# Fox scores and all value products on full rows and columns, masks in fp32r, banks cleared by VectorE, all operands at one residue modulo 256 bytes

## The chip, the cores and the metric

The kernel runs on one core of a Trainium2 chip. The metric is the device time in microseconds (us) of one execution. TensorE (PE) multiplies matrices, VectorE (DVE), ScalarE (ACT) and GpSimd (POOL) work element by element, SyncE (SP) issues loads. PEld is PE's loading of weights, the stationary operand of a product; the other operand streams through the array, column by column.

## The reference

A trunk of two layers on 512 frames of 1,024 numbers, in fp32. Layer 0 has two groups of heads side by side: 8 heads of latent attention (MLA) and 8 heads of stick-breaking attention. Layer 1 has 16 heads of forgetting attention, called Fox here. After each mixer come a layer norm, a gated feed-forward (SwiGLU, 2,816 wide), another norm, and a gated embedding.

```python
# stick-breaking, one query block
past = s[None, :] < t[:, None]
z = einsum('bhqd,bhkd->bhqk', q_blk, k) * SB_DIM ** -0.5
log_rem = where(past, log_sigmoid(-z), 0.0)
between = cumsum(log_rem, axis=3, reverse=True) - log_rem
att = where(past, exp(log_sigmoid(z) + between), 0.0)
o = einsum('bhqk,bhkd->bhqd', att, v)
# forgetting attention (Fox), one query block
causal = s[None, :] <= t[:, None]
logits = einsum('bhqd,bhkd->bhqk', q_blk, k) * FOX_DIM ** -0.5 + d_t[..., :, None] - dcum[..., None, :]
w = softmax(where(causal, logits, -inf))
o = einsum('bhqk,bhkd->bhqd', w, v)
# each mixer: x = LN(alpha x + mixer(x)); x = LN(alpha x + SwiGLU(x)); x = x + sigmoid(gate(x)) * embedding
```

## The kernel before

PE works in a rounded fp32 type, fp32r. To keep the accuracy of fp32 each operand is split in a high and a low part (whi and wlo for weights, xTh and xTl for the transposed x, pth and ptl for the transposed weights of an attention), and each product is the sum of three: high by low, high by high, low by high (mm3). In a name such as ps_h<-xTl,whi the tile before the arrow is the bank of PSUM that is written, and the others are what is read.

The attentions put the two parts of 64-wide heads side by side. The queries of a head are a tile of 128 rows: the high part in the head's own 64 rows and the low part in the other 64. The keys of the head have the high part in both halves. So one pass of 128 rows (the second pass) gives two of the three products. The third, high query by low key, is the low pass: it takes the low keys kl, which lie in the head's own 64 rows only, and so contracts 64 rows. Both passes are qk_products. One kl tile of [128, 512] holds the low keys of both heads of a pair, 64 rows each.

A causal mask is added on PE as one more product: the identity times a tile with large negative numbers where the mask forbids. Identity (identb) and masks are bf16. For values (add_values) one product has 128 weight columns, the high and the low part of a head's values, and streams pth; the next has 64 columns, the high part alone, and streams ptl into rows 0 to 63 of the same bank. finish_head adds the two halves of the bank.

A stick-breaking head adds into a part of its bank with each key block, so the bank is cleared first: by a product of 512 columns with a tile of zeros.

One Fox unit is a head and a query block of 128 (16 heads x 4 = 64 units): scores, one step later its softmax (DVE, ACT), later the transposes (PE) and the products with the values. An MLA unit is the same without the bias. Fox handles two heads as a pair, whose queries and keys are projected by project_qk one pair ahead. In the gaps between the steps, fill generators hand PE dense products: projections (ps_qkT, ps_v) and outputs (ps_y). The order on each engine is made when the program is built. Tiles come from pools: kl, pth and ptl take turns in the seven buffers of "pT"; a tile has to wait for the last read of the one before it in its buffer.

Constants and long-lived tiles (identity, masks, neg_tri, neg_ones, x, xTh, xTl) are laid one after another in SBUF, and the pools (pieces of weights, qkT, kl, gT, oT, pth, ptl) behind them. Among them are two tiles of one fp32 column, minus_half and bf, that take 32 bytes each. In the built program xTh and xTl begin at 160 modulo 256 bytes, identity, masks and neg tiles at 128, and every tile of the pools at 192.

Of the kernel before, what the change touches and what calls it, by code (L numbers as in the profile page):

```python
# [10 lines left out]
BF16 = mybir.dt.bfloat16  # L11
# [4 lines left out]
P = 128  # L16
S = 512
NT = S // P
# [14 lines left out]
HD = 64  # L33
# [3 lines left out]
# From here on softplus(z) is z in float32, and exp(z) is still finite.  # L37
SOFT_CAP = 60.0

# Column offsets of the blocks of a causal [rows, keys] map that is stored without its empty part.  # L40
# [6 lines left out]
def trunk(ctx: ExitStack, tc: tile.TileContext, a, out):  # L47
# [13 lines left out]
    # ---------------------------------------------------------------- buffers  # L61
# [23 lines left out]
    # ---------------------------------------------------------------- constants  # L85
    ident = const.tile([P, P], F32, name="ident")
    make_identity(nc, ident)
    identb = const.tile([P, P], BF16, name="identb")
    nc.gpsimd.tensor_copy(identb, ident)

    def mask_tile(name):
        t = const.tile([P, P], BF16, name=name)
        nc.gpsimd.memset(t, 0.0)
        return t

    # [query, key]: keys after the query
    mask_fox = mask_tile("mask_fox")
    nc.gpsimd.affine_select(mask_fox, mask_fox, [[-1, P]], ALU.is_ge, NEG, 0, 1)
    # [key, query]: keys at or after the query
    mask_sb = mask_tile("mask_sb")  # L100
    nc.gpsimd.affine_select(mask_sb, mask_sb, [[1, P]], ALU.is_gt, NEG, 0, -1)
    zeros = mask_tile("zeros")
# [5 lines left out]
    # [key', key]: -1 where key' >= key  # L108
# [3 lines left out]
    minus_half = const.tile([P, 1], F32, name="minus_half")  # L112
# [6 lines left out]
    # ---------------------------------------------------------------- helpers  # L119
    def split(hi, lo, src, scale=1.0, eng=None):  # L120
        """hi + lo == scale * src, each with 12 significant bits."""
        if isinstance(scale, float) and scale == 1.0:
            nc.scalar.copy(hi, src)
            (eng or nc.vector).tensor_tensor(lo, src, hi.bitcast(F32), ALU.subtract)
        else:
            nc.scalar.mul(hi, src, scale)
            nc.vector.scalar_tensor_tensor(lo, src, scale, hi.bitcast(F32), ALU.mult, ALU.subtract)

    # engines that take the high and the low part of weights in turn
# [6 lines left out]
    def wload(src, n, m):  # L136
        """A weight piece [128, n x m] as its two parts, each [128, n, m]."""
# [49 lines left out]
    def layer_norm(t, sums, g, b):  # L187
        """x[t] normalised in place; sums are those of its halves."""
# [22 lines left out]
    def row_weights(w, rows):  # L211
        """Whole rows of weights, as addressed by project_block."""
        pieces = [row_piece(w, r) for r in rows]
        return lambda i, half: both(pieces[i], lambda v: v[:, 0, half * S:(half + 1) * S])

    def project_block(t, lhs, w, first, ps_of, sums=(None, None), halves=(0, 1)):
        """x[t] (+)= [lhs tiles]^T @ w; w(i, half) are the two parts of the weights. A generator, one step per half."""
# [8 lines left out]
    def store_values(ps):  # L226
        """8 heads of values of one token block, per head the two parts side by side: [128, 8 x (64 | 64)]."""
# [5 lines left out]
    def store_part(vals, t, part, ps):  # L233
        """Keeps 4 heads of values of a token block: vals[t, part // 2] holds 8 heads."""
# [5 lines left out]
    def x_values(vals, part, src, ps_of, more=None):  # L240
        """4 heads of values, all frames: vals[frame block, part // 2] holds 8 heads. A generator.
        more, of columns [frame, block, n], takes the products with the further columns of src."""
# [13 lines left out]
    # ---------------------------------------------------------------- work for the gaps of the attention  # L256
    class Fill:
        """Generators of matrix products, emitted a little at a time between the steps of an attention."""
# [48 lines left out]
    def project_qk(dst, hp, i, src, kind, twice):  # L307
        """Transposed, split queries (i = 0, scaled) or keys (i = 1) of two heads, from rows 0:64 and 64:128.

        dst[hp][:, j] has both parts of the queries of head j, the high one in its own rows; dst[hp][:, 2 + j]  # L310
        twice the high part of its keys (the copy by twice[j]); low_keys has the low part in its own rows."""
# [4 lines left out]
        else:  # L316
            low_keys[kind, hp] = act.tile([P, S], F32R, tag="pT", bufs=7, name="kl")
# [6 lines left out]
        for j in range(2):  # L324
# [5 lines left out]
            else:  # L330
# [5 lines left out]
                dve.tensor_tensor(low_keys[kind, hp][own], ps[own], hi.bitcast(F32), ALU.subtract)  # L336

    def qk_products(o, kind, hp, q, k, j, keys_first):
        """The three products of the parts of q and k, each (tile, column, slice), of head j of two, in two passes."""
        own = slice(j * HD, (j + 1) * HD)  # L340
        (qt, qc, qs), (kt, kc, ks) = q, k
        passes = [(qt[own, qc, qs], low_keys[kind, hp][own, ks]), (qt[:, qc, qs], kt[:, kc, ks])]
# [4 lines left out]
    def project_out(w_out, fours, outs, first):  # L347
        """Adds the heads of outs to x: w_out[half, c] are the weights of four heads, outs[2 c] and outs[2 c + 1]."""
# [14 lines left out]
    def finish_rows(lhs, w, first, norm, between=lambda t: None, after=lambda t: None):  # L363
        """The last addend of x, its norm, and the transposes; between(t) emits work for the waits."""
# [17 lines left out]
    def split_pair(both_heads, room=None):  # L382
        """The two parts; in room[0] and room[1] where x^T isn't needed any more."""
# [12 lines left out]
    def add_values(o_ps, kb, pt, val, h, first, last):  # L396
        """Adds a key block: rows 0:64 take both parts of pt with the high part of val, 64:128 its low part."""
        th, tl = pt
        c = h * 2 * HD
        nc.tensor.matmul(o_ps[:, kb * P:], lhsT=val[:, c:c + 2 * HD], rhs=th, start=first, stop=False,  # L400
                         skip_group_check=True)
        nc.tensor.matmul(o_ps[0:HD, kb * P:], lhsT=val[:, c:c + HD], rhs=tl, start=False, stop=last,
                         skip_group_check=True)

    # ---------------------------------------------------------------- softmax attention
# [3 lines left out]
    def softmax_attention(n_pairs, head, mask, outs, fill, ns, kind, norm_engines, room):  # L409
        """head(hp, j) gives scores(qb, ps), bias(qb) or None, values by key block, and the head among them.  # L410

        Step by step: scores of one query block; its weights one step later; their transposes five, and the
        products with the values six steps later. norm_engines by query block; room gives places of outs."""
# [22 lines left out]
        def scores(u):  # L436
# [10 lines left out]
            if mask is not None:  # L447
                nc.tensor.matmul(u.s[:, u.n - P:u.n], lhsT=identb, rhs=mask, start=False, stop=True)

        def weights(u):  # L450
# [6 lines left out]
            else:  # L457
# [3 lines left out]
                # the row's own term, in the maximum as in the logits  # L461
# [44 lines left out]
    # ---------------------------------------------------------------- stick-breaking attention  # L506
    def stick_attention(n_pairs, pair, vals, outs, fill, ns, kind, room):
        """pair(hp) gives the projected queries and keys of two heads; vals are the value blocks.

        Scores are kept [key, query]; key blocks run from the last to the first. Step by step: softplus of  # L510
        one block, one step later its weights, and three steps later their products with the values."""
# [11 lines left out]
        def scores(u):  # L523
# [5 lines left out]
            nc.tensor.matmul(u.z[:, 0:P], lhsT=identb, rhs=mask_sb, start=False, stop=True)  # L529
# [575 lines left out]
```

## Time and profile before

| | |
|---|---|
| time, median of 3 runs | 1426.98 us (1425.24 to 1427.11) |
| span of the profiled execution | 1425.5 us |
| PE busy | 1396.9 us, 98% of the span |
| DVE, ACT, POOL busy | 56%, 43%, 28% |

The profile gives the span of one execution; the runs give a time each. The first attention (MLA and stick-breaking) ends around 282 us, the feed-forward and gate of layer 0 run to about 736, the Fox attention to about 960, and the feed-forward of layer 1 to the end.

### The profile page before, as it was taken

The numbers are of one execution on the slowest core, as the hardware profiler recorded it, in microseconds if no ns is written. First come the engines' busy times: TensorE is split into PE (matmuls) and PEld (weight loads), VectorE is DVE, ScalarE is ACT, GpSimd is POOL, SyncE is SP. The second block draws the span as 40 slices with busy tenths as digits, with TensorE's granted clock in tenths as the row PEclk, the third lists the DMA queues.
The fourth block names the chain that finished last, engine by engine and source line by source line (L and its number), as shares of the span: only waits on it lengthen the run. The fifth ranks groups of instructions, "written<-read, shape, count | busy, mean of one in ns | idle before, by whom it ended". The sixth has DMA issues, their size and how long they took to land.

```text
span 1425.5 us, 18859 instructions
## 1 busy us (share of the span) xinstructions
PE 1396.9 (98%) x6784; PEld 1129.2 (79%) x6784; DVE 793.8 (56%) x1481; ACT 607.3 (43%) x1261; POOL 401.9 (28%) x400
## 2 busy tenths in 40 slices
PE   8999999799999999999989999999999999999998
PEld 7888777588888888887877788778888888888877
DVE  4655789833444444448636665698434444444485
ACT  4666776542322232324446564665422223232242
POOL 5654732221111111112144443442211111111130
PEclk9999999999999999999999999999999999999999
DMA  6211412142232333331233222122423232322212
GB/s 229 91 41 40 129 53 89 60 133 74 89 102 93 104 101 97 96 103 60 83 116 111 79 81 68 45 82 92 138 74 103 92 105 92 106 94 95 98 60 96
DMA packets 69166, 131.75 MB, mean 92 GB/s; under 512 B 8128, under 2 KB 8896, under 8 KB 69056
## 3 DMA queue, kind: packets, MB, share of 16 engines
q1 hardware_dynamic: 66304, 120.75, 26.3%
q0 software_dynamic: 2768, 9.80, 2.0%
q8 instruction: 53, 0.87, 0.3%
q14 instruction: 41, 0.34, 0.1%
HBM read 127.80 MB, written 2.72 MB: 92 GB/s over the span
## 4 chain that ended last, share of the span: by engine, by line
PE 91%; DVE 4%; DMA 2%; ACT 2%; issue 1%; SPq 0%; POOL 0%; DVEq 0%; POOLq 0%; ACTq 0%
PE ps_h L151 12%; PE ps_h L153 12%; PE ps_h L152 12%; PE ps_y L151 7%; PE ps_y L152 7%; PE ps_y L153 7%; PE ps_s L345 3%; PE ps_qkT L151 3%; PE ps_qkT L152 3%; PE ps_qkT L153 3%; PE ps_g L153 2%; PE ps_g L151 2%; PE ps_g L152 2%; PE ps_t L434 2%; PE ps_z L539 1%; PE ps_v L151 1%
## 5 line engine op out<-in xcount | busy, mean ns | idle before, releaser
L147 POOL TENSOR_TENSOR wlo<-wraw,whi 128x512 fp32r<-128x512 f32 (+2 forms) x212 | 276.6, 1312 | 777.4 <-ACT whi L146 648.4
L146 ACT CAST whi<-wraw 128x512 fp32r<-128x512 f32 (+1 forms) x402 | 237.7, 616 | 577.4 <-PE ps_h L152 263.6
L152 PE MATMUL ps_h<-xTh,whi 128*128 128x512 f32 (+1 forms) x736 | 283.9, 386 | 0.0
L151 PE MATMUL ps_h<-xTl,whi 128*128 128x512 f32 (+1 forms) x736 | 283.9, 386 | 0.0
L153 PE MATMUL ps_h<-xTh,wlo 128*128 128x512 f32 (+1 forms) x736 | 283.8, 386 | 0.0
L147 DVE TENSOR_TENSOR wlo<-wraw,whi 128x512 fp32r<-128x512 f32 (+1 forms) x215 | 172.1, 816 | 134.9 <-ACT whi L146 133.3
L209 DVE TENSOR_TENSOR x<-x,ps_y 128x512 f32<-128x512 f32 x176 | 119.8, 683 | 151.8 <-PE ps_y L153 151.7
L153 PEld LDWEIGHTS ps_h<-xTh,wlo 128*128 128x128 f32 x736 | 138.3, 188 | 30.4
L152 PEld LDWEIGHTS ps_h<-xTh,whi 128*128 128x128 f32 x736 | 138.3, 188 | 30.2
L151 PEld LDWEIGHTS ps_h<-xTl,whi 128*128 128x128 f32 x736 | 138.2, 188 | 30.3
L152 PE MATMUL ps_y<-whi,gT 128*128 128x512 f32 x352 | 137.1, 390 | 0.0
L151 PE MATMUL ps_y<-wlo,gT 128*128 128x512 f32 x352 | 137.1, 391 | 0.0
L153 PE MATMUL ps_y<-whi,gT 128*128 128x512 f32 x352 | 136.2, 389 | 0.0
L666 DVE TENSOR_TENSOR silu<-silu,ps_h 128x512 f32<-128x512 f32 x44 | 30.3, 688 | 121.8 <-PE ps_h L153 119.4
L151 PE MATMUL ps_qkT<-xTl,whi 128*128 128x512 f32 x192 | 79.1, 412 | 2.1 <-DVE fu L916 0.9
L152 PE MATMUL ps_qkT<-xTh,whi 128*128 128x512 f32 x192 | 77.6, 404 | 0.0
L151 PEld LDWEIGHTS ps_y<-wlo,gT 128*128 128x128 f32 x352 | 66.1, 188 | 14.4
L153 PE MATMUL ps_qkT<-xTh,wlo 128*128 128x512 f32 x192 | 77.4, 403 | 0.0
L153 PEld LDWEIGHTS ps_y<-whi,gT 128*128 128x128 f32 x352 | 66.1, 188 | 14.2
L152 PEld LDWEIGHTS ps_y<-whi,gT 128*128 128x128 f32 x352 | 66.1, 188 | 14.2
L151 PE MATMUL ps_v<-wlo,xTh 128*128 128x256 f32 (+1 forms) x192 | 56.4, 295 | 3.3 <-DVE wlo L147 3.2
L152 PE MATMUL ps_v<-whi,xTh 128*128 128x256 f32 (+1 forms) x192 | 55.2, 289 | 0.0
(234 smaller groups left out, 2513.0 us busy)
## 6 DMA issues: line engine op xcount, KB each, us to landing
wraw<-in_ffn_w_dram SPq DMA_DIRECT2D x264, 256.0 KB, 2.8
wraw<-in_w_gate_dram SPq DMA_DIRECT2D x32, 256.0 KB, 2.9
wraw<-in_w_qkf_dram SPq DMA_DIRECT2D x32, 256.0 KB, 2.9
wraw<-in_w_qkb_dram SPq DMA_DIRECT2D x16, 256.0 KB, 3.0
wraw<-in_a_w_out_dram SPq DMA_DIRECT2D x16, 256.0 KB, 2.7
kbias<-nd_dram POOLq DMA_DIRECT2D x8, 512.0 KB, 5.0
wraw<-in_c_w_out_dram SPq DMA_DIRECT2D x16, 256.0 KB, 2.9
wraw<-in_w_vf_dram SPq DMA_DIRECT2D x15, 256.0 KB, 3.1
```

What stands on the lines that cost most here:

```text
L146: (eng_hi.copy if eng_hi is acts else eng_hi.tensor_copy)(hi[:, c:end], raw)
L147: eng_lo.tensor_tensor(lo[:, c:end], raw, hi[:, c:end].bitcast(F32), ALU.subtract)
L151: nc.tensor.matmul(o, lhsT=lhs[0], rhs=rhs[1], start=first, stop=False)
L152: nc.tensor.matmul(o, lhsT=lhs[0], rhs=rhs[0], start=False, stop=False)
L153: nc.tensor.matmul(o, lhsT=lhs[1], rhs=rhs[0], start=False, stop=last)
L209: nc.vector.tensor_tensor(xs, xs, ps, ALU.add)
L345: nc.tensor.matmul(o, lhsT=lhsT, rhs=rhs, start=n == 0, stop=False)
L434: nc.tensor.transpose(u.ps[:, blk(qb - u.i)], u.h.pr[:, QOFF[qb] + u.i * P:QOFF[qb] + (u.i + 1) * P], ident)
L539: nc.tensor.matmul(u.z[:, c:u.n], lhsT=w, rhs=rhs, start=False, stop=i == len(mms) - 1, skip_group_check=True)
L666: nc.vector.tensor_tensor(s, s, hps[1], ALU.mult)
```

## The change

It has five parts. No computation of the reference is left out; where 128 rows or columns take the place of 64, a product of two low parts is added to the sum.

1. The identity and the masks are fp32r (identr, mask_fox, mask_sb); each is built in a scratch tile and copied. The transposes read identr as fp32.
2. The stick-breaking bank is cleared by a memset of VectorE.
3. For Fox (both_halves), each head of a pair has its own kl tile. Its own 64 rows are written as before and then copied to the other 64, by ACT for the first head and by GpSimd for the second. The low pass contracts 128 rows. The stick-breaking heads keep one kl tile for each pair and 64 rows.
4. Both value products have 128 weight columns.
5. minus_half and bf become columns of a tile of 32 fp32 (128 bytes). In the built program xTh, xTl, x and every tile of the pools then begin at 0 modulo 256 bytes; identr, masks, neg tiles and the columns tile begin at 128.

```diff
+LINE = 32
-    ident = const.tile([P, P], F32, name="ident")
-    make_identity(nc, ident)
-    identb = const.tile([P, P], BF16, name="identb")
-    nc.gpsimd.tensor_copy(identb, ident)
+    identr = const.tile([P, P], F32R, name="identr")
+    raw_ident = temp("scratch")[:, 0:P]
+    make_identity(nc, raw_ident)
+    nc.vector.tensor_copy(identr, raw_ident)
+    ident = identr.bitcast(F32)
-    def mask_tile(name):
-        t = const.tile([P, P], BF16, name=name)
-        nc.gpsimd.memset(t, 0.0)
+    def mask_tile(name, *select):
+        raw = temp("scratch")[:, 0:P]
+        nc.gpsimd.memset(raw, 0.0)
+        nc.gpsimd.affine_select(raw, raw, *select)
+        t = const.tile([P, P], F32R, name=name)
+        nc.vector.tensor_copy(t, raw)
-    zeros = mask_tile("zeros")
-    minus_half = const.tile([P, 1], F32, name="minus_half")
+    columns = const.tile([P, LINE], F32, name="columns")
+    minus_half = columns[:, 0:1]
...
-            low_keys[kind, hp] = act.tile([P, S], F32R, tag="pT", bufs=7, name="kl")
+            low_keys[kind, hp] = [act.tile([P, S], F32R, tag="pT", bufs=7, name="kl") for _ in range(1 + both_halves)]
...
-                dve.tensor_tensor(low_keys[kind, hp][own], ps[own], hi.bitcast(F32), ALU.subtract)
+                low = low_keys[kind, hp][j if both_halves else 0]
+                dve.tensor_tensor(low[own], ps[own], hi.bitcast(F32), ALU.subtract)
+                if both_halves:
+                    (acts.copy if j == 0 else gps.tensor_copy)(low[other], low[own].bitcast(F32))
...
-        passes = [(qt[own, qc, qs], low_keys[kind, hp][own, ks]), (qt[:, qc, qs], kt[:, kc, ks])]
+        low = low_keys[kind, hp]
+        rows, low = (slice(0, P), low[j]) if len(low) == 2 else (slice(j * HD, (j + 1) * HD), low[0])
+        passes = [(qt[rows, qc, qs], low[rows, ks]), (qt[:, qc, qs], kt[:, kc, ks])]
...
-        nc.tensor.matmul(o_ps[:, kb * P:], lhsT=val[:, c:c + 2 * HD], rhs=th, start=first, stop=False,
-                         skip_group_check=True)
-        nc.tensor.matmul(o_ps[0:HD, kb * P:], lhsT=val[:, c:c + HD], rhs=tl, start=False, stop=last,
-                         skip_group_check=True)
+        for n, t in enumerate(pt):
+            nc.tensor.matmul(o_ps[:, kb * P:], lhsT=val[:, c:c + 2 * HD], rhs=t, start=first and n == 0,
+                             stop=last and n == 1, skip_group_check=True)
...
-                nc.tensor.matmul(u.s[:, u.n - P:u.n], lhsT=identb, rhs=mask, start=False, stop=True)
+                nc.tensor.matmul(u.s[:, u.n - P:u.n], lhsT=identr, rhs=mask, start=False, stop=True)
...
-            nc.tensor.matmul(u.z[:, 0:P], lhsT=identb, rhs=mask_sb, start=False, stop=True)
+            nc.tensor.matmul(u.z[:, 0:P], lhsT=identr, rhs=mask_sb, start=False, stop=True)
...
-                nc.tensor.matmul(h.o_ps, lhsT=zeros,
-                                 rhs=zeros.rearrange("p (o m) -> p o m", o=1).broadcast_to([P, NT, P]),
-                                 start=True, stop=False, skip_group_check=True)
+                nc.vector.memset(h.o_ps, 0.0)
...
-        bf = const.tile([FOX_H, 1], F32, name="bf")
+        bf = columns[0:FOX_H, 1:2]
```

What the change moves in the order: the first piece is PE in the Fox attention, one unit's scores with a value projection around it, before:

```order
L345 MATMUL ps_s<-kl,qkT 128x512
L345 MATMUL ps_s<-qkT 128x512
L448 LDWEIGHTS identb
L448 MATMUL ps_s<-mask_fox,identb 128x128
L151 MATMUL ps_v<-wlo,xTh 128x256
L152 MATMUL ps_v<-whi,xTh 128x256
L153 MATMUL ps_v<-whi,xTl 128x256
L402 MATMUL ps_o<-ptl,val 64x512
L400 MATMUL ps_o<-pth,val 128x384
```

and the same unit in the changed kernel, where the line numbers are those of its own code:

```order
L353 MATMUL ps_s<-kl,qkT 128x512
L408 MATMUL ps_o<-pth,val 128x512
L353 MATMUL ps_s<-qkT 128x512
L454 MATMUL ps_s<-mask_fox,identr 128x128
L155 MATMUL ps_v<-whi,xTh 128x256
L156 MATMUL ps_v<-whi,xTl 128x256
L408 MATMUL ps_o<-ptl,val 128x512
L440 MATMUL ps_t<-identr,prob 128x128
L408 MATMUL ps_o<-pth,val 128x384
```

The mask has no weight load of its own row any more, ptl's product writes 128 rows of the bank where it wrote 64, and a product of pth has moved in between the two passes.

The second piece is ACT in the Fox attention of the changed kernel, around the keys of a pair (L335 and L339 write the high keys, L343 the copy of the low keys of the first head):

```order
L470 ACTIVATE prob,sm<-prob,nb 128x512
L335 CAST qkT<-ps_qkT 64x512
L339 CAST qkT<-ps_qkT 64x512
L343 CAST kl<-kl 64x512
L335 CAST qkT<-ps_qkT 64x512
L126 CAST val<-ps_v 128x4x64
L126 CAST pth<-ps_t 128x128
```

L343 is new; what stood behind it stands behind it still.

The third piece is DVE in the stick-breaking attention of the changed kernel, where a head's bank is cleared (sp is the softplus of the scores ps_z, val the low part of values):

```order
L388 TENSOR_TENSOR o<-ps_o,o_low 64x512
L577 TENSOR_SCALAR sp<-ps_z 128x512
L127 TENSOR_TENSOR val<-ps_v,val 128x4x64
L552 MEMSET ps_o 128x512
L577 TENSOR_SCALAR sp<-ps_z 128x128
L587 TENSOR_TENSOR sp<-ps_z,sp 128x512
```

The memset is new on DVE, between the end of one head (L388) and the softplus of a later block; the other rows stand as before.

## Rows read from the trace of the kernel before

**Rows 1.** The page: the chain that ended last, by engine.
```profile
PE 91%; DVE 4%; DMA 2%; ACT 2%; issue 1%; SPq 0%; POOL 0%; DVEq 0%; POOLq 0%; ACTq 0%
```

**Rows 2.** Windows: start:end, length, busy us (count) by engine, PE's granted clock, DMA share, GB/s.
```profile
12.00:228.00 216.00, 214.09 (x1203) 174.40 (x1202) 142.63 (x289) 137.05 (x336) 115.05 (x113) 1.00 0.28 87
228.00:282.00 54.00, 45.45 (x210) 33.55 (x208) 44.85 (x100) 31.31 (x75) 10.67 (x14) 0.94 0.23 73
282.00:700.00 418.00, 417.47 (x1879) 341.06 (x1878) 197.02 (x281) 133.15 (x232) 74.45 (x67) 1.00 0.30 95
746.00:960.00 214.00, 213.64 (x1157) 165.12 (x1156) 142.93 (x413) 123.29 (x299) 91.21 (x91) 1.00 0.24 80
```

**Rows 3.** Timeline of PE, three streams' ends: start us, us, engine, line, out<-in, shapes.
```profile
330.02 0.40 PE L151 MATMUL ps_h<-xTl,whi 128*128 128x512 f32 x1
...
336.79 0.40 PE L153 MATMUL ps_h<-xTh,wlo 128*128 128x512 f32 x1
...
337.25 0.39 PE L152 MATMUL ps_y<-whi,gT 128*128 128x512 f32 x1
...
339.52 0.39 PE L153 MATMUL ps_y<-whi,gT 128*128 128x512 f32 x1
...
680.18 0.39 PE L152 MATMUL ps_g<-whi,xTh 128*128 128x512 f32 x1
...
682.51 0.39 PE L153 MATMUL ps_g<-whi,xTl 128*128 128x512 f32 x1
```

**Rows 4.** Timeline of PE, a Fox unit behind an output product.
```profile
900.84 0.39 PE L153 MATMUL ps_y<-whi,oT 128*128 128x512 f32 x1
901.16 0.49 PE L345 MATMUL ps_s<-kl,qkT 64*128 64x512 f32 x1
901.58 0.50 PE L345 MATMUL ps_s<-qkT 128*128 128x512 f32 x1
901.92 0.23 PE L448 MATMUL ps_s<-mask_fox,identb 128*128 128x128 bf16 x1
901.96 0.48 PE L400 MATMUL ps_o<-pth,val 128*128 128x512 f32 x1
902.28 0.40 PE L402 MATMUL ps_o<-ptl,val 128*64 128x512 f32 x1
902.51 0.34 PE L400 MATMUL ps_o<-pth,val 128*128 128x384 f32 x1
```

**Rows 5.** Lines by shape, PE: count | busy us, mean ns | idle before.
```profile
L152 PE MATMUL ps_h<-xTh,whi 128*128 128x512 f32 x672 | 265.8, 396 | 0.0
L152 PE MATMUL ps_qkT<-xTh,whi 128*128 128x512 f32 x192 | 77.6, 404 | 0.0
L152 PE MATMUL ps_g<-whi,xTh 128*128 128x512 f32 x120 | 47.5, 396 | 0.0
```

**Rows 6.** Lines by shape, DVE and POOL, in the projection of keys.
```profile
L336 DVE TENSOR_TENSOR kl<-ps_qkT,qkT 64x512 fp32r<-64x512 f32 x24 | 16.4, 685 | 9.5 <-ACT qkT L335 6.8 <-ACT qkT L331 2.5
L333 POOL CAST qkT<-qkT 64x512 fp32r<-64x512 f32 x8 | 4.9, 608 | 3.4 <-ACT qkT L331 3.1
```

**Rows 7.** Timeline of PE, narrow fp32r products in a stick-breaking head.
```profile
47.13 0.22 PE L539 MATMUL ps_z<-spp,neg_tri 128*128 128x128 f32 x1
47.19 0.39 PE L539 MATMUL ps_z<-spp,neg_ones 128*128 128x128 f32 x2
47.42 0.33 PE L539 MATMUL ps_z<-spp,neg_tri 128*128 128x256 f32 x1
```

**Rows 8.** Lines, PEld: the mask's weights and those of Fox's second pass.
```profile
L448 PEld LDWEIGHTS <-identb 128*128 128x128 bf16 x64 | 6.1, 96 | 5.1 <-issue 2.4
L345 PEld LDWEIGHTS ps_s<-qkT 128*128 128x128 f32 x64 | 11.9, 186 | 9.4 <-issue 6.5
```

**Rows 9.** Lines, PE: the value products of ptl and the clearing products.
```profile
L402 PE MATMUL ps_o<-ptl,val 128*64 128x128 f32 (+3 forms) x128 | 42.2, 333 | 0.3 <-DVE ptl L124 0.2
L546 PE MATMUL ps_o<-zeros 128*128 128x512 bf16 x8 | 3.4, 445 | 2.1 <-POOL zeros L93 2.1
```

More of the change, by code (lines that the diff above doesn't have):

```diff
@@ L10 @@
 F32R = mybir.dt.float32r
-BF16 = mybir.dt.bfloat16
 AF = mybir.ActivationFunctionType
@@ L83, in trunk @@
     ps_at, ps_o, ps_pq = bank("at", 4), bank("o", 2), bank("pq", 2)
-    ident = const.tile([P, P], F32, name="ident")
-    make_identity(nc, ident)
-    identb = const.tile([P, P], BF16, name="identb")
-    nc.gpsimd.tensor_copy(identb, ident)
-    def mask_tile(name):
-        t = const.tile([P, P], BF16, name=name)
-        nc.gpsimd.memset(t, 0.0)
-        return t
[L97 to L101, printed above, removed]
-    zeros = mask_tile("zeros")
+    identr = const.tile([P, P], F32R, name="identr")
[9 more added lines that the diff above has]
+        nc.vector.tensor_copy(t, raw)
+        return t
+    mask_fox = mask_tile("mask_fox", [[-1, P]], ALU.is_ge, NEG, 0, 1)
+    mask_sb = mask_tile("mask_sb", [[1, P]], ALU.is_gt, NEG, 0, -1)
     scratch = temp("scratch")
@@ L305, in trunk, with project_qk @@
     low_keys = {}
-    def project_qk(dst, hp, i, src, kind, twice):
+    def project_qk(dst, hp, i, src, kind, twice, both_halves):
         piece = wload(src, KT, P)
@@ L335, in project_qk @@
                     (acts.copy if twice[j] is acts else dve.tensor_copy)(dup, ps[own])
-                dve.tensor_tensor(low_keys[kind, hp][own], ps[own], hi.bitcast(F32), ALU.subtract)
+                low = low_keys[kind, hp][j if both_halves else 0]
+                dve.tensor_tensor(low[own], ps[own], hi.bitcast(F32), ALU.subtract)
+                if both_halves:
+                    (acts.copy if j == 0 else gps.tensor_copy)(low[other], low[own].bitcast(F32))
     def qk_products(o, kind, hp, q, k, j, keys_first):
-        own = slice(j * HD, (j + 1) * HD)
         (qt, qc, qs), (kt, kc, ks) = q, k
-        passes = [(qt[own, qc, qs], low_keys[kind, hp][own, ks]), (qt[:, qc, qs], kt[:, kc, ks])]
+        low = low_keys[kind, hp]
+        rows, low = (slice(0, P), low[j]) if len(low) == 2 else (slice(j * HD, (j + 1) * HD), low[0])
+        passes = [(qt[rows, qc, qs], low[rows, ks]), (qt[:, qc, qs], kt[:, kc, ks])]
         for n, (qa, ka) in enumerate(passes):
@@ L396, in add_values @@
     def add_values(o_ps, kb, pt, val, h, first, last):
-        th, tl = pt
         c = h * 2 * HD
-        nc.tensor.matmul(o_ps[:, kb * P:], lhsT=val[:, c:c + 2 * HD], rhs=th, start=first, stop=False,
-                         skip_group_check=True)
-        nc.tensor.matmul(o_ps[0:HD, kb * P:], lhsT=val[:, c:c + HD], rhs=tl, start=False, stop=last,
-                         skip_group_check=True)
+        for n, t in enumerate(pt):
+            nc.tensor.matmul(o_ps[:, kb * P:], lhsT=val[:, c:c + 2 * HD], rhs=t, start=first and n == 0,
+                             stop=last and n == 1, skip_group_check=True)
     class Unit:
@@ L861, in add_qb @@
             for i in range(2):
-                fill.add(("qb", hp, i), project_qk(qk_b, hp, i, w_qk[i, hp], "b", (dve, dve)), after)
+                fill.add(("qb", hp, i), project_qk(qk_b, hp, i, w_qk[i, hp], "b", (dve, dve), False), after)
         add_qb(0)
@@ L928, in mixer_fox @@
             for i in range(2):
-                fill.add(("q", hp, i), project_qk(qk, hp, i, a["w_qkf"][i, hp], "f", (acts, gps)),
+                fill.add(("q", hp, i), project_qk(qk, hp, i, a["w_qkf"][i, hp], "f", (acts, gps), True),
                          [("scores_f", hp - 2)] if hp >= 2 else [])
```

## The prediction

> **What bounds the kernel now.** I read the chain of work that ended last first [rows 1]: 91% of the span is TensorE (PE), DVE has 4%. So I asked, stage by stage, whether PE is busy from end to end [rows 2]. It is in the feed-forward stages (417.47 of 418 us), in the Fox attention (213.64 of 214 us) and nearly so in the first attention up to 228 us (214.09 of 216). It is not in the tail of layer 0, from 228 to 282 us: 45.45 of 54 us, with DVE at 44.85. A PE nanosecond saved is therefore a nanosecond of span everywhere but in that tail. "Busy" only says that some matmul is under way, not that the array streams at its peak. The next view was therefore the timeline of PE, start to start: what matters is how long after one matmul's start the next one starts, since the durations (390 to 500 ns) overlap.
>
> Two plain streams give the yardstick [rows 3]. Twenty-nine steps of ps_h (512 columns each) take 336.79 - 330.02 = 6.77 us, 233.4 ns each. Ten steps of ps_y from gT take 2.27 us, 227 ns each. Shape, type and clock are the same. What differs is where the operands lie: x^T (xTh, xTl) lies at 160 modulo 256 bytes in the built program, the pieces of weights and gT at 192. ps_h has one operand at each, ps_y both at 192. ps_g, with x^T as its weights and a piece of weights streaming as in ps_y, takes 2.33 us for ten steps, 233 each. ps_qkT has an operand in x^T as well.
>
> A Fox unit costs more than its stream [rows 4]. I measure each start against 0.227 us for 512 columns. From the last ps_y to the 64-row low pass: 0.32 (0.09 too much). From the low pass to the 128-row pass: 0.42 (0.19). From there to the bf16 mask: 0.34 (0.11). The mask's own slot is 0.04. From the 128-column product of pth to the 64-column one of ptl: 0.32 (0.09); from ptl on, 0.23, nothing lost.
>
> **The change part by part.**
>
> *Residue.* In the changed kernel x^T and all pieces of weights, keys, gT and oT lie at 0 modulo 256; the constants (identr, masks, neg_tri, neg_ones) at 128. It costs no instruction. Matmuls of 512 columns with one operand in x^T: 3 lines x (672 + 192 + 120) = 2,952 [rows 5]. I price each at the difference of the two streams, 6 ns (6.4 by the two stretches; the low end is nothing, if the residues have no part in it). 2,952 x 6 ns = 17.7 us, and about 1.3 us for the narrower ones, by the same share: 19.0 us. The upper end is in the third rival.
>
> *Fox low pass on 128 rows.* 64 units lose the entry and the exit, (0.09 + 0.19) x 64 = 17.9 us. The row supports it as far as it goes: wherever 128 rows follow 128 rows no such gap stands. The pass itself streams the same number of columns. For it ACT makes 8 and POOL 8 copies of 64x512. Nearest rows [rows 6]: the same kind of copy takes POOL 608 ns, DVE's subtraction before it 685 ns. So 8 x 0.6 = 4.9 us on each of two engines that do not bound Fox (ACT 123.29 and POOL 91.21 of 214 us, [rows 2]). They lie one head pair ahead of their use: in the changed order at least 25 PE instructions stand between the last key projection of a pair and the first use of ACT's copy, and 72 before that of POOL's, which is 4 us or more against 1.3 us for subtraction and copy. If that cover were gone, 16 x 1.3 = 21 us would show. ACT's queue holds, behind such a copy, the next qkT cast, a value cast and a pth cast (second order piece): each is 0.6 us later, and pth releases a product on PE. I keep 1 us for that.
>
> *Masks in fp32r.* The 0.11 us before the mask goes 64 times in Fox (7.0 us) and 32 times in the stick-breaking part, 8 heads of 4 key blocks (3.5 us). The fp32r mask is not free: a 128-column fp32r product after a wider one takes 47.19 - 47.13 = 0.06 us against 0.04, so 0.02 x 96 = 1.9 us come off. Two 128-column ones in a row take (47.42 - 47.19)/2 = 0.115 each [rows 7]. The first query block of each Fox head has low pass, second pass and mask at 128 columns, so 16 heads x 3 x 0.055 = 2.6 us are lost. Net 6.0 us: Fox 7.0 - 1.3 - 2.6 = 3.1, stick 2.9. The low end is nothing (the wait belongs to the mask and not to its type).
>
> The weight load argues against this part. PE's weight loads of the bf16 identity take 96 ns, of an fp32r tile 186 [rows 8]; 96 x 0.09 = 8.6 us, if they were exposed. In the plain streams such loads stand in front of every matmul and the spacing stays at 0.227, so behind a matmul of 256 columns or more they are hidden. The Trainium skill ("TensorE: Matmul & The Clock Gate", section on the weight-path perf modes) says that the fast weight load is for weights that are not fp32, and the trace agrees (96 against 186 ns). By that rule alone, with every load exposed, the masks would lose 8.6 us in place of the 2.6 above, and 43 us below would be 37.
>
> *Value products on 128 columns.* 128 products [rows 9]. The adjacent pair shows 0.09; most have other work between and show little, since only the change of width is taken away. I take a third, 0.03 x 128 = 4 us, between nothing and 128 x 0.09 = 11.5. PE streams the same number of columns, so nothing is added; finish_head reads the same tile.
>
> *Banks cleared by VectorE.* Eight bf16 products of 512 columns leave [rows 9]. Two stand ahead of all work. Six take a slot of a 512-column product each, 0.227 x 6 = 1.4 us. DVE gets eight writes of 128x512; the nearest row is 685 ns, so 0.7 us each. Where they stand DVE is 66% busy (142.63 of 216, [rows 2]); behind one stands a softplus step (first-stage sp, third order piece), 0.7 us late, and it feeds work three steps ahead. Its cover is the projection work that fills PE. Without it 6 x 0.7 = 4 us.
>
> *Sum.* 19.0 + 17.9 + 6.0 + 4 + 1.4 = 48.3 us. Two deductions. In the tail of layer 0, PE waits for the DVE and ACT chain, so what the residue, the masks and the value products save there becomes idle time; I count 3 us. And buffers: kl takes two of the seven "pT" buffers for each pair where it took one, and pth and ptl turn over in the rest. By the order the nearest re-use moves from 14 matmuls to 15, but 15 places instead of 13 lie under 25. With the ACT copies that is 2 us. Left: 43.3, say 43. Against the profiled span of 1425.5 that is 1382.5. The median of the runs, 1426.98, stands 1.5 above that span, so **1384 us** by the runs.
>
> **The rivals.**
>
> *The residues have no part in it.* The 6 ns may come from the operation (ps_h alternates its two halves of weights, ps_y its addend) or from the read of x^T, and stay. For: ps_y and ps_h differ in more than the address. Against: ps_g streams the same kind of tile as ps_y into the same kind of bank, differs in where its weights lie, and takes the 233 of ps_h [rows 3]. Time: 1384 + 19 = 1403. A rule in the skill would give this end: "SBUF — State Buffer", section on specifications, names lines of 16 bytes. By that rule 160, 192 and 0 are all starts of a line, and this part gives nothing; no row here tests lines of any size.
>
> *A full row count does not remove the waits of the Fox pass.* The 0.09 and 0.19 could be the change of buffers, banks or weights instead of 64 rows against 128. Then 17.9 us stay: 1402. Against: pth after the mask, and ps_y's own steps, also change tile and bank and show none.
>
> *The common residue 0 is better than the common 192.* 512 columns at 2.4 GHz are 213.3 ns; ps_y's 227 is 13.7 above it. If two operands at 0 reached that floor, 2,952 products would gain another 13.7 ns, 40 us, and ps_y and the Fox products would add some 10: about 1334. For: no stream here has both operands at 0, so nothing excludes it; against: two operands at one residue, 192, already stand at 227 [rows 3]. The skill ("TensorE: Matmul & The Clock Gate", section on the back-to-back issue gap) measures 215.7 ns for such a gap; by that rule the time would come out near 1340, and the trace's 227 does not agree with it.
>
> *Slower: the seven buffers.* If two kl tiles for each pair leave too few for pth and ptl, each of the 64 Fox units waits for the last read of an earlier one. ACT or DVE then wait at the head of their queues, and PE for pth. It turns the sign from 43/64 = 0.7 us a unit; a full chain of cast (0.6) and subtraction (0.7) that is no longer covered is 1.3 us, 83 us in all: about 1467. Against: PE idles 0.36 us in the whole Fox window [rows 2], and 15 matmuls, 3 us, lie between the last read and the next in the closest case.
>
> **How the numbers follow.** Forecast 0.70, first rival 0.13, second 0.05, third 0.05, buffers 0.03; 0.04 for part-way cases between 1403 and no change. The forecast's own range is 1370 to 1397: the value products' ends (+4, -7), the residue's (by 6 to 7 ns, half lost), and the granted clock: in the tail of layer 0 it was 0.94 [rows 2], which is 3 us that can shift with any idle time. The range of 8 in 10 takes in the first two rivals and leaves the third and fourth out: 1366 to 1405. About 0.2% (3 us) is what a measurement of this kernel can tell from no change. All cases but the buffers and the end of the part-way ones are faster by far more: faster 0.95, same 0.02, slower 0.03.
>
> **What would show it.** Residue: ps_h at 227 ns by the same count of 29 steps; 233 says the first rival, under 220 the third. Fox: from low pass to second pass 0.23, into the low pass 0.23, second pass to mask 0.23, mask slot 0.06; gaps of 0.4 would say the second rival. Stage by stage: 282 to 700 shorter by some 13 us, Fox by some 25, the stretch before 228 by some 6, the tail unchanged. Buffers: PE waits for pth or ptl in Fox, tens of us together, would make the sign wrong. A DVE chain in the stick heads that makes PE wait for sp after each clearing would cost up to 4 us.

## The result and the profile after

The changed kernel takes 1401.55 us (median of 4 runs, 1401.39 to 1402.54) against 1427.05 for the kernel before in the same runs: ratio 0.9823, 95% interval 0.9809 to 0.9838, so 25.5 us less. The forecast was 1384, with a range of 1366 to 1405. The sign and the range hold; of the 43 us forecast 25.5 came. The time lies where the first two rivals put it (1403 and 1402), and neither is what happened.

The page of the profiled execution, engines and chain by engine [rows 1]:

```profile
PE 1361.1 (97%) x6776; PEld 1139.6 (81%) x6776; DVE 797.0 (57%) x1492; ACT 611.6 (44%) x1269; POOL 408.8 (29%) x406
PE 85%; DVE 7%; ACT 3%; DMA 3%; issue 2%; POOL 1%; SPq 0%; DVEq 0%; POOLq 0%; ACTq 0%
```

PE is busy 36 us less than before, and its share of the chain fell from 91 to 85%; DVE's rose from 4 to 7%. Not all that PE saved became span: something else ends last in places.

The streams that the prediction named first. Timeline of PE of the changed kernel, first and last step of a run of ps_h [rows 3]:

```profile
324.62 0.39 PE L156 MATMUL ps_h<-xTh,wlo 128*128 128x512 f32 x1
...
335.28 0.39 PE L155 MATMUL ps_h<-xTh,whi 128*128 128x512 f32 x1
```

There are 47 steps in 10.66 us, 226.8 ns each, where 233.4 stood. The Fox unit behind an output product, on the same view [rows 4]:

```profile
879.59 0.39 PE L156 MATMUL ps_y<-whi,oT 128*128 128x512 f32 x1
879.82 0.39 PE L353 MATMUL ps_s<-kl,qkT 128*128 128x512 f32 x1
880.04 0.40 PE L353 MATMUL ps_s<-qkT 128*128 128x512 f32 x1
880.27 0.23 PE L454 MATMUL ps_s<-mask_fox,identr 128*128 128x128 f32 x1
880.34 0.44 PE L408 MATMUL ps_o<-pth,val 128*128 128x512 f32 x1
880.62 0.39 PE L408 MATMUL ps_o<-ptl,val 128*128 128x512 f32 x1
```

The steps 0.32, 0.42 and 0.34 have become 0.23, 0.22 and 0.23. The mask's slot grew from 0.04 to 0.07. The step from the product of pth to that of ptl is 0.28 where 0.32 stood.

A unit in the stick-breaking heads, where the mask is fp32r too, but the low pass still has 64 rows:

```profile
64.56 0.28 PE L156 MATMUL ps_v<-whi,xTl 128*128 128x256 f32 x1
64.78 0.49 PE L353 MATMUL ps_z<-qkT,kl 64*128 64x512 f32 x1
65.20 0.51 PE L353 MATMUL ps_z<-qkT 128*128 128x512 f32 x1
65.54 0.22 PE L535 MATMUL ps_z<-mask_sb,identr 128*128 128x128 f32 x1
```

The same unit in the kernel before:

```profile
65.41 0.49 PE L345 MATMUL ps_z<-qkT,kl 64*128 64x512 f32 x1
65.83 0.49 PE L345 MATMUL ps_z<-qkT 128*128 128x512 f32 x1
66.17 0.23 PE L529 MATMUL ps_z<-mask_sb,identb 128*128 128x128 bf16 x1
```

In both the second pass comes 0.42 us after the low pass and the mask 0.34 after the second pass, whether the mask is fp32r or bf16. The gap ahead of the mask did not go with the mask's type. This is the first step of the forecast that the trace contradicts.

Where the span moved, by marks in the two timelines: the last output product of layer 0's mixer starts at 268.52 us (before: 269.07), the last ps_y of the feed-forward of layer 0 at 651.92 (659.24), the first scores of Fox at 741.52 (749.07), the last value product of Fox at 950.22 (973.59), the last transposes of the norm behind Fox at 988.83 (1006.11). So layer 0's mixer gained 0.6 us, the feed-forward of layer 0 6.8, Fox 15.8, and what stands from those last transposes to the end of the span, which is layer 1's feed-forward, 8.2. The 32.5 us from Fox's last value product to the last transposes became 38.6: 6.1 us were given back there. With 0.2 us between the feed-forward and Fox these make the 25.5. Windows of the changed kernel: the three that [rows 2] show, then Fox and what follows it, each in its new place:

```profile
12.00:228.00 216.00, 213.64 (x1199) 178.17 (x1198) 143.98 (x297) 137.25 (x338) 115.14 (x113) 1.00 0.27 87
228.00:282.00 54.00, 45.45 (x208) 34.09 (x207) 44.41 (x99) 31.33 (x74) 10.66 (x14) 0.94 0.22 72
282.00:700.00 418.00, 417.08 (x1912) 346.74 (x1911) 203.34 (x289) 136.16 (x237) 75.81 (x67) 1.00 0.29 95
741.50:950.20 208.70, 205.75 (x1221) 180.00 (x1220) 155.86 (x439) 132.74 (x320) 99.59 (x100) 1.00 0.26 86
950.20:988.80 38.60, 33.29 (x169) 27.50 (x168) 26.23 (x43) 19.29 (x36) 12.00 (x16) 0.91 0.21 72
```

Fox and the stretch behind it in the kernel before, by the same marks:

```profile
749.07:973.59 224.52, 224.16 (x1212) 173.60 (x1212) 154.74 (x438) 129.29 (x313) 94.38 (x93) 1.00 0.24 79
973.60:1006.10 32.50, 32.47 (x172) 27.19 (x171) 29.15 (x46) 20.91 (x39) 12.65 (x18) 1.00 0.27 90
```

Before, PE was busy from end to end in that last stretch at full clock. Now it idles there for 5.3 us, and the mean granted clock is 0.91. The view of waits and the timeline of PE in that stretch name them:

```profile
PE ps_xt L179 <- DVE x L201: 2.4, 1, 2.4
PE ps_e L154 <- DVE x L210: 1.8, 1, 1.8
PE ps_y L154 <- ACT xTh L126: 1.1, 1, 1.1
```

```profile
965.91 1.15 PE L179 MATMUL ps_xt<-identr,x 128*128 128x128 f32 x8 [2.42 <-DVE x L201]
968.85 0.80 PE L154 MATMUL ps_e<-wlo,pTh 128*128 128x512 f32 x1 [1.78 <-DVE x L210]
969.44 0.63 PE L155 MATMUL ps_e<-whi,pTh 128*128 128x512 f32 x1
969.87 0.63 PE L156 MATMUL ps_e<-whi,pTl 128*128 128x512 f32 x1
```

An output product waits for ACT, and then the norm's chain on DVE makes PE wait twice. Behind the last of these waits the products of 512 columns start 0.43 us apart, which is the 1.2 GHz level (the view of windows has a granted clock of 0.50 from 968.85 to 973.50 us). After about 973.7 us the steps are 0.23 again.

### The profile page after: what moved, and what is told of

It reads as the page before. It is cut to its first block, busy times and chain, and to the rows that moved or that the text cites. A ratio compares the mean times of both kernels' runs of the same rounds, so it can differ in the third digit from the quotient of the medians.

```text
span 1400.0 us, 18875 instructions
## 1 busy us (share of the span) xinstructions
PE 1361.1 (97%) x6776; PEld 1139.6 (81%) x6776; DVE 797.0 (57%) x1492; ACT 611.6 (44%) x1269; POOL 408.8 (29%) x406
## 4 chain that ended last, share of the span: by engine, by line
PE 85%; DVE 7%; ACT 3%; DMA 3%; issue 2%; POOL 1%; SPq 0%; DVEq 0%; POOLq 0%; ACTq 0%
PE ps_h L154 11%; PE ps_h L155 11%; PE ps_h L156 11%; PE ps_y L154 7%; PE ps_y L155 7%; PE ps_y L156 7%; PE ps_qkT L154 2%; PE ps_qkT L155 2%; PE ps_qkT L156 2%; PE ps_o L408 2%; PE ps_g L154 2%; PE ps_g L156 2%; PE ps_g L155 2%; PE ps_z L545 1%; PE ps_t L440 1%
## 5 line engine op out<-in xcount | busy, mean ns | idle before, releaser
L154 PE MATMUL ps_h<-xTl,whi 128*128 128x512 f32 (+1 forms) x736 | 279.7, 380 | 0.0
L155 PE MATMUL ps_h<-xTh,whi 128*128 128x512 f32 (+1 forms) x736 | 279.5, 380 | 0.0
L156 PE MATMUL ps_h<-xTh,wlo 128*128 128x512 f32 (+1 forms) x736 | 279.3, 380 | 0.0
```

Source lines behind the costliest of these rows:

```text
L154: nc.tensor.matmul(o, lhsT=lhs[0], rhs=rhs[1], start=first, stop=False)
L155: nc.tensor.matmul(o, lhsT=lhs[0], rhs=rhs[0], start=False, stop=False)
L156: nc.tensor.matmul(o, lhsT=lhs[1], rhs=rhs[0], start=False, stop=last)
```

## The experiments

My theory from these rows: the residues and the row count of the Fox pass work by themselves; the gap ahead of the mask belongs to the 64-row pass and not to the mask's type; and the end of Fox gives back what is saved there, since the dense products are used up before the chain of the last heads and the norm. The rivals stand in each expectation. The times of "before" are those measured beside each group of kernels.

**The residues alone.** The kernel before with

```diff
-    minus_half = const.tile([P, 1], F32, name="minus_half")
+    columns = const.tile([P, 32], F32, name="columns")
+    minus_half = columns[:, 0:1]
...
-        bf = const.tile([FOX_H, 1], F32, name="bf")
+        bf = columns[0:FOX_H, 1:2]
```

> The kernel before with the two narrow tiles made columns of one of 128 bytes, and nothing else: x^T and the pools' tiles all at 0 modulo 256. Theory A (the residues cost time by themselves): ps_h at 227 ns a step instead of 233, 18 us over all matmuls, time 1409 (1407 to 1412). Rival (the 6 ns belong to another part of the change): ps_h stays at 233, time 1427.

1410.72 us against 1426.76, ratio 0.9889 (0.9874 to 0.9904): 16.0 us less. Timeline of PE, ps_h, 30 steps from the first row to the last:

```profile
322.15 0.39 PE L154 MATMUL ps_h<-xTh,wlo 128*128 128x512 f32 x1
...
328.95 0.39 PE L154 MATMUL ps_h<-xTh,wlo 128*128 128x512 f32 x1
```

6.80 us, 226.7 ns each. The rival is out. By the marks, 7.8 us came in the feed-forward of layer 0, 8.0 in that of layer 1 and 0.9 between the first of these and Fox; layer 0's mixer ended 0.8 us later than before and Fox took 224.1 us where it took 224.5. In the attentions the ps_qkT steps also fell, from 233 ns to 228 in layer 0 and 230 in Fox in the mean, and the stretches hardly got shorter for it.

**Everything but the residues.** The changed kernel with minus_half and bf as tiles of their own again.

> The changed kernel with the old residues (minus_half and bf tiles of their own). If the residue's part simply adds: 1401.5 + 18 = 1419 to 1420. If the slower stream of PE hides the waits at the end of Fox again, part of that comes back: 1412 to 1417.

1418.89 us, ratio to before 0.9946 (0.9929 to 0.9963). Against the 1401.55 of the changed kernel that is 17.3 us, so the residue's part adds to the others. The slower stream does not hide the waits at the end of Fox: the stretch behind it is 38.3 us here as well.

**Which residues count.** The changed kernel with 64, and with 128, bytes between x and the pools (16 columns of pad in the first, 32 in the second):

```diff
     x = [const.tile([P, D], F32, name=f"x{t}") for t in range(NT)]
+    pad = const.tile([P, 16], F32, name="pad")
+    nc.vector.memset(pad, 0.0)
```

> The changed kernel with 64 bytes between x and the pools: x^T at 0 and every tile of the pools at 64 modulo 256 bytes. If any two unlike residues modulo 256 cost 6 ns: ps_h 233, ps_y 227, time 1416 to 1418. If only the residue modulo 64 (or 32) counts: ps_h 227, time 1401 to 1402.

> The changed kernel with 128 bytes between x and the pools: x^T at 0, every tile of the pools at 128 modulo 256. The run with 64 bytes between took back the gain in the feed-forward. If unlike residues modulo 256 cost the 6 ns: ps_h 233, time 1415 to 1417. If it is the residue modulo 128 that counts: ps_h 227, time 1401 to 1403.

1415.71 us (ratio to before 0.9919, 0.9902 to 0.9935) and 1418.8 (0.9938, 0.9923 to 0.9953). Timelines of PE, ps_h, 30 steps, with 64 and then with 128 bytes:

```profile
322.19 0.39 PE L157 MATMUL ps_h<-xTh,whi 128*128 128x512 f32 x1
...
329.19 0.39 PE L157 MATMUL ps_h<-xTh,whi 128*128 128x512 f32 x1
```

```profile
322.17 0.40 PE L158 MATMUL ps_h<-xTh,wlo 128*128 128x512 f32 x1
...
329.15 0.40 PE L158 MATMUL ps_h<-xTh,wlo 128*128 128x512 f32 x1
```

233.3 and 232.7 ns: for ps_h, operands 64 and 128 bytes apart cost the same 6 ns as 32 bytes in the kernel before. In ps_g, where x^T is the weights, they do not all cost the same. Its longest run with 64 bytes, 95 steps from the first row to the last:

```profile
682.31 0.40 PE L157 MATMUL ps_g<-whi,xTh 128*128 128x512 f32 x1
...
704.07 0.40 PE L156 MATMUL ps_g<-wlo,xTh 128*128 128x512 f32 x1
```

That is 229.0 ns a step. The same run takes 232.3 ns with 128 bytes, 233.3 in the kernel before (32 bytes) and 227.2 in the changed kernel. ps_y from gT, with both operands in the pools, has a median step of 227 ns in all four. (Identity, masks and neg tiles begin at 128 in all of these kernels; "all operands" in the title leaves them out.) So equal residues modulo 256 are the best of those tried, and what an unlike pair costs depends on the distance and on which operand lies where; why, no run here tells. The times lie 0.3 us under the first range and 1.8 over the second; in the two traces, whose spans are 5.3 us apart, 2.9 of these lie in layer 0's mixer, which ends at 268.56 us with 64 bytes and at 271.41 with 128. The Trainium skill ("SBUF — State Buffer", section on specifications) gives lines of 16 bytes; all of 0, 64, 128, 160 and 192 begin one, and by that rule alone none of these kernels should differ. They do, by the steps just shown, and the measurement decides.

**Fox's low pass alone on 128 rows.** The kernel before with the three hunks on kl and qk_products from the change.

> The kernel before with only the low pass of Fox on 128 rows (two kl tiles, the copies); masks bf16, old residues. Theory A (all three gaps of a Fox unit come from the switch between 64 and 128 rows): the steps into the low pass, to the second pass and from there to the bf16 mask all fall to about 0.23 for 512 columns; gross 18 + 6 us, less up to 8 us that the end of Fox gives back: 1403 to 1412. Theory B (the gap ahead of the mask belongs to the mask's type): that step stays at 0.34, gross 18 us, 1409 to 1418.

1416.29 us, ratio 0.9932 (0.9917 to 0.9947): 10.5 us less. The mechanism is theory A's; the time misses A's range by 4 us and lies in the one that I gave B. Timeline of PE, a unit with the bf16 mask:

```profile
886.93 0.39 PE L153 MATMUL ps_y<-whi,oT 128*128 128x512 f32 x1
887.16 0.39 PE L350 MATMUL ps_s<-kl,qkT 128*128 128x512 f32 x1
887.39 0.39 PE L350 MATMUL ps_s<-qkT 128*128 128x512 f32 x1
887.62 0.23 PE L453 MATMUL ps_s<-mask_fox,identb 128*128 128x128 bf16 x1
```

All steps are 0.23, the one to the bf16 mask too. Fox took 209.1 us instead of 224.5, and the stretch behind it 38.2 instead of 32.5: 15.4 us won, 5.7 given back at once.

**The masks alone in fp32r.** The kernel before with identr and the two masks from the change.

> The kernel before with only the masks and the identity in fp32r; low pass on 64 rows, old residues. Theory A: the gap ahead of the mask stays at 0.34, and the mask's slot is 0.02 to 0.05 us longer in 96 places: 1427 to 1432. Theory B (the prediction's): the gap falls to 0.23 in Fox and in the stick-breaking heads, 1419 to 1423.

1427.71 us, ratio 1.0006 (0.9996 to 1.0015). Theory A. Timeline of PE, a unit, and the weight loads of the mask from the view of lines:

```profile
901.58 0.49 PE L349 MATMUL ps_s<-kl,qkT 64*128 64x512 f32 x1
902.00 0.50 PE L349 MATMUL ps_s<-qkT 128*128 128x512 f32 x1
902.34 0.22 PE L452 MATMUL ps_s<-mask_fox,identr 128*128 128x128 f32 x1
```

```profile
L452 PEld LDWEIGHTS ps_s<-mask_fox,identr 128*128 128x128 f32 x64 | 12.1, 189 | 0.1
```

0.34 to the mask, with or without bf16. The load takes 189 ns instead of 96 [rows 8]. Counted over the timeline of Fox, the steps out of the masks are longer by 1.7 us together, and the time of the run can't be told from no change. So the rule that the prediction weighed against the masks ("TensorE: Matmul & The Clock Gate" of the Trainium skill, section on the weight-path perf modes) is seen in the load, and its price with every load exposed (8.6 us) is not seen in the time.

**The value products alone, and the banks alone.** The kernel before with add_values of the change; the kernel before with the memset in place of the zeros product.

> The kernel before with only both value products on 128 columns. Prediction's term: 4 us over 128 products, 1423. Rival (the 0.09 after a product of pth belongs to the change of the streamed tile and the bank, or is taken by what stands between): no gain, 1426 to 1428.

> The kernel before with only the banks cleared by VectorE. The prediction's term: 1.4 us to the good, 1425.5. If layer 0 is set by DVE and ACT and gives such gains back before its end: 1426.5 to 1428.

1429.28 us against 1427.39, ratio 1.0017 (1.0007 to 1.0026); and 1429.16 against 1427.42, ratio 1.0014 (1.0004 to 1.0023). Neither gains; both cost about 2 us, near the limit of what the runs can tell, and both lie a little past the ranges of their rivals (up to 1428). Why they cost it was not settled. Apart, the five parts sum to 21.9 us of gain (16.0 and 10.5, less 1.0, 1.9 and 1.7), together they gave 25.5; where the 3.6 us between come from, no run tells.

**The stick-breaking heads on 128 rows too.** The changed kernel with

```diff
-project_qk(qk_b, hp, i, w_qk[i, hp], "b", (dve, dve), False)
+project_qk(qk_b, hp, i, w_qk[i, hp], "b", (dve, dve), True)
```

> The changed kernel with the low pass of the stick-breaking heads on 128 rows too (two kl tiles for each pair, copied by ACT and GpSimd). Theory A (all gaps, the one ahead of the mask too, come from 64 against 128 rows): the steps low pass to second pass and second pass to mask fall to 0.23 in the stick-breaking heads too, 32 x 0.4 = 13 us gross; what of it is kept is what layer 0 keeps at all: if PE sets its end, 1389 to 1393, if its end is set by DVE and ACT, 1398 to 1402. Theory B (the gap there belongs to the mask or to the heads' own order): the steps stay.

1406.41 us, ratio to before 0.9855 (0.984 to 0.9869): 4.9 us slower than the changed kernel. Timeline of PE, a stick-breaking unit:

```profile
63.48 0.28 PE L156 MATMUL ps_v<-whi,xTl 128*128 128x256 f32 x1
63.59 0.40 PE L353 MATMUL ps_z<-qkT,kl 128*128 128x512 f32 x1
63.83 0.39 PE L353 MATMUL ps_z<-qkT 128*128 128x512 f32 x1
64.06 0.22 PE L535 MATMUL ps_z<-mask_sb,identr 128*128 128x128 f32 x1
```

The steps fell to 0.24 and 0.23, as theory A says: the row count sets them here as well, and the fp32r mask takes part in neither kernel. But layer 0's mixer ended at 275.02 us instead of 268.52. The view of waits of PE from 12 to 270 us, the three largest of 18:

```profile
PE ps_lt L746 <- DVE o L388: 2.1, 2, 1.3
PE ps_z L353 <- ACT att L581: 1.7, 4, 0.6
PE ps_kr L773 <- DVE kr L766: 1.6, 1, 1.6
```

PE waits in many places for many tiles of DVE, ACT and GpSimd: the 18 waits come to 13.9 us, where the changed kernel has six that come to 5.3. Both ranges of the expectation are missed: I had a gain or nothing, and it was a loss. That the two copies and the one buffer more for each pair load engines that already set the end is my reading; no run takes the copies apart from the buffers.

**The end of Fox.** The changed kernel with 1700 instead of 1800 ns of dense products handed out in a Fox step:

```diff
-        for _ in softmax_attention(8, fox_head, mask_fox, outs, fill, lambda s: 1800, "f",
+        for _ in softmax_attention(8, fox_head, mask_fox, outs, fill, lambda s: 1700, "f",
```

> The changed kernel with 1700 instead of 1800 ns of dense products handed to PE in each step of Fox. In the order, 60 products instead of 47 then stand between the last value product and the first transposes of the norm, 45 instead of 27 between those and the next ps_h. Theory A (the end of Fox gives back up to 8 us since the dense products are used up ahead of the chain of the last heads and the norm, which then PE waits for at a falling clock): those waits go, 1394 to 1397. Rival (the end is set by DVE, which a gentler fill doesn't speed up): 1400 to 1403.

1397.97 us, ratio to before 0.9793 (0.9779 to 0.9808); the changed kernel had 0.9823 (0.9809 to 0.9838). Window of PE from the last value product of Fox to the last transposes behind it:

```profile
951.10:983.50 32.40, 32.30 (x172) 27.12 (x171) 29.08 (x46) 20.84 (x39) 12.77 (x18) 1.00 0.28 93
```

The stretch is back at 32.4 us, PE full, the clock at 1.00. So the 6.1 us there came of which products are left to cover the chain, and not of DVE's speed. Of the 6.1 us 3.6 reached the span, since Fox itself took 211.3 us instead of 208.7. (The expectation has 47 products between Fox's last value product and the first transposes in the changed kernel; its trace has 51. Before, and with 1700, there are 60.) The waits of Fox with 1700 are for DVE and ACT; the view of waits there:

```profile
PE ps_qkT L154 <- DVE kl L341: 1.6, 1, 1.6
PE ps_o L408 <- DVE ptl L127: 1.5, 2, 1.1
PE ps_y L154 <- DVE x L208: 1.2, 2, 0.7
PE ps_s L353 <- ACT kl L343: 1.0, 2, 0.5
```

**Without the value products; and with less on DVE.** The first takes the kernel with 1700 and gives it add_values as before. The second:

```diff
-        for _ in softmax_attention(8, fox_head, mask_fox, outs, fill, lambda s: 1800, "f",
-                                   [gps, gps, dve, dve], ...
+        for _ in softmax_attention(8, fox_head, mask_fox, outs, fill, lambda s: 1750, "f",
+                                   [gps, gps, gps, dve], ...
```

> The changed kernel with 1700 ns of fill for each Fox step and the value products as they were before, ptl on 64 columns. Theory A (128 columns are worth nothing or cost a little, as the run with that part alone says by +1.9): 1395 to 1398. The prediction's term (4 us to the good for 128 columns): 1401 to 1403.

> The changed kernel with 1750 ns of fill for each Fox step and the third query block of a Fox head normalised by GpSimd instead of VectorE; in the order the end of Fox has 60 and 45 products again, as with 1700. If the waits that are left inside Fox (7 us with 1700, mostly for results of DVE) come from DVE's load: they halve, 1393 to 1396. If they come from the chain's length and not from its load, or GpSimd becomes late: 1398 to 1402.

1396.73 us, ratio 0.9783 (0.9768 to 0.9797): the value products on 128 columns are worth nothing here either. And 1392.72 us, ratio 0.9752 (0.9736 to 0.9769): the best version of all, 34.7 us under the kernel before. The view of waits has 2.3 us in Fox, where the run with 1700 has 5.3 (not the 7 of the expectation). Window of Fox in it:

```profile
744.00:950.00 206.00, 203.73 (x1215) 178.31 (x1214) 143.66 (x423) 133.04 (x320) 119.37 (x116) 1.00 0.27 86
```

DVE has 143.66 us of work where the changed kernel has 155.86; GpSimd took it (119.37 against 99.59). Fox is 205.7 us long between its marks and the stretch behind it 32.4. Two knobs moved here (the fill and the engine), so how much each gave is not told apart; the direction fits the waits for DVE that the run with 1700 showed.

## Why the prediction was right, and where it was off

The range holds in part by luck: it was made that wide for the first two rivals, and neither took place.

- *Residue, 19.0 us.* Right. 16.0 alone and 17.3 on top of the rest, by the step of 6 ns that was forecast. Nearly all of it is from the feed-forward stages. The first rival is out. So is the third: with both operands at 0 the step is 226.8 ns, and the 227 of two operands at 192 was already the best of these kernels. (The 215.7 ns that this rival takes from the Trainium skill, "TensorE: Matmul & The Clock Gate", stand there in the section on what each phase is for; the section that it names has about 216 ns for an isolated gap. No stream here shows either.)
- *Fox's low pass, 17.9 us, and the masks in Fox, 3.1 net.* The gaps of 0.09, 0.19 and 0.11 all went, in the run with the pass alone; the second rival is out. But I had put the 0.11 down to the bf16 mask. The run with masks alone (no gain) and the run with rows alone (gap gone at a bf16 mask) show that it belongs to the switch from 64 to 128 rows, and is seen at the second product after it. So the 0.11 was priced in the right place by a wrong cause. Counted from start to start over Fox in both timelines, against 0.227 us for 512 columns, the steps into the low pass, from it to the second pass and from there to the mask were too long by 7.6, 11.7 and 6.3 us together before, and are by 0.4, 2.5 and 1.2 now. That is 21.5 us; 2.0 come off it, by which the steps out of the masks grew. So 19.5 us came where the two terms had 17.9 + 3.1 = 21.0: the size was nearly right.
- *Masks in the stick-breaking heads, 2.9 us.* Wrong for the same reason: their low pass still has 64 rows, so the gap stayed. The run with 128 rows there shows it closing.
- *Value products, 4 us, banks, 1.4 us.* Wrong in sign, both: apart they measure about +2 us each, not -5.4 together. The 0.09 between pth and ptl in [rows 4] is one adjacent case, and a third of it over 128 products was my choice, not a row. In the timeline of Fox before, 11 such pairs stand side by side, and they are 0.45 us too long in all.
- *Layer 0.* I kept about 6 us of its mixer and got 0.6, no more than the kernel with the Fox rows alone, which changes nothing there (268.40 us). A busy share of 214.09 of 216 us let me treat it as bound by PE up to 228 us. In the run with stick-breaking rows, PE's gaps closed there and the mixer ended 6.5 us later, with waits for DVE, ACT and GpSimd; in the run with residues alone its steps got shorter and it ended no earlier. So it is not PE alone that sets its end; what does, beside those waits, stays open. And the deduction of 3 us for the tail of layer 0 was too small.
- *The 2 us for buffers and queues.* The fourth rival didn't come: the waits for kl in Fox are 0.4 us, and the view of waits in Fox names no other place of that kind. But I looked for a stall in each unit and not at the end of the stage. There 6.1 us were lost: the chain of the last heads and the norm did not get faster, the dense products that covered it had been moved ahead, PE waited 5.3 us for DVE and ACT and then ran for some 4.7 us at the lower clock. The run with 1700 shows it by undoing it. This is the largest loss that the sum had no term for.

Summed by the stretches that the prediction named (13 us in the feed-forward, 25 in Fox, 6 ahead of 228 us): the products behind the 13 are those of both layers' feed-forwards, and I gave them to the stretch of the first alone; they came as 6.8 and 8.2. Layer 0's mixer lacks 5.4 us, Fox 9.2, and the end of Fox gave back 6.1; 44 + 2 - 5.4 - 9.2 - 6.1, and 0.2 between the feed-forward and Fox, is the 25.5 measured.

Most of Fox's 9.2 can be counted in the two timelines. The two terms above brought 1.5 us less than forecast; the view of waits has 2.9 us in Fox where 0.4 stood; nine output products that stood behind Fox's last value product stand ahead of it now (141 of ps_y in Fox against 132, 2.0 us); and the value products gave nothing, where half of their 4 us was meant for Fox. That is 8.0 us; the last 1.2 are not told.

## What to carry to other kernels

Price a gap only after asking which instruction *two* places back changed shape: the product that shows the gap need not cause it. When a stage gets shorter, check what its end was covered by, since the chain of norms and last heads behind it is as long as before and the products that hid it may have gone ahead; a smaller fill gave 3.6 us here, while shorter steps of PE in layer 0, bought with copies, cost 4.9. And "PE is busy 99%" over overlapping matmuls does not prove that PE sets a stage's end; a run that shortens its steps does.

## What was not expected of the hardware

Two operands of a matmul at unlike residues modulo 256 bytes (32, 64 and 128 apart) took 233 ns for 512 columns, at like residues (both at 0, both at 192) 227; only with x^T as the weights and 64 bytes between them was it 229. A product of 128 rows behind one of 64 rows came 0.42 us after it instead of 0.23, and the mask behind that was late by 0.11 us again, whether bf16 or fp32r.
